# Opening norm of a two-layer encoder: sums of squares by TensorE as the input lands, scale on ScalarE, shifted tiles in PSUM

## The chip, the cores and the metric

The kernel runs on one core of a Trainium2 chip. The metric is the time of one execution on the device in microseconds (us); lower is better. The core has TensorE (PE in the profile, its weight loads PEld), VectorE (DVE), ScalarE (ACT), GpSimd (POOL) and SyncE (SP), which here only issues DMA transfers. SBUF is the working memory, PSUM the memory that TensorE writes and that VectorE and ScalarE can read and write.

## The reference, cut to what matters

Two layers; each is a half-step feed-forward network (FFN), a mixer of three branches, and another FFN. Each sub-layer starts with an RMS norm with a shift and a scale that come from a second input `c`. Only the very first of these norms, in front of the first FFN, is touched here.

```python
def rms_norm(x, gain):
    y = xf * lax.rsqrt(jnp.mean(xf * xf, axis=-1, keepdims=True) + EPS)
    return y * gain
def modulate(h, shift, scale):
    return h * (1 + scale[:, None, :]) + shift[:, None, :]
def swiglu(h, w_gate, w_up, w_down):
    return (jax.nn.silu(h @ w_gate) * (h @ w_up)) @ w_down
...
c_act = jax.nn.silu(c)
for l in range(DEPTH):
    mod = (c_act @ w_ada[l] + b_ada[l]).reshape(B, N_MOD, D_MODEL)
    h = modulate(rms_norm(x, norm_gain[l, 0]), mod[:, 0], mod[:, 1])
    x = x + 0.5 * mod[:, 2][:, None, :] * swiglu(h, ffn_w_gate[l, 0], ffn_w_up[l, 0], ffn_w_down[l, 0])
    ...
```

Sizes: 512 tokens, 1024 features, FFN width 2816, two layers, all float32.

## The kernel before, in words

Features lie on the 128 partitions, tokens along the free axis, so `x` is 8 feature tiles of 128 x 512. Float32 precision is kept in the large products by splitting both operands into a high and a low part: `hi` is the value rounded to the matmul format fp32r, `lo` the rest. A product is then three matmuls (`triple`, L117 to L122): hi x hi (L119), hi x lo and lo x hi (L120, L121).

Weights come through `wchunk` (L237): a DMA on SP's queue into `raw` (2 buffers), a cast on ScalarE into `whi` (L262, 3 buffers), and a subtraction into `wlo` (L264, 3 buffers), on VectorE or, with `lo_eng`, on GpSimd.

The modulation vectors are made by `mod_step` (L190) one 128-feature piece at a time: a DMA brings a 128 x 1024 piece of `w_ada` (4 buffers, tag `v2`), and one VectorE instruction (L196) multiplies it by the broadcast silu(c) and sums along the row, with the bias added. For the scale pieces (kind 1) a small instruction (L201) makes `apre` = (1 + scale) x gain.

The opening (L132 to L151, then `Ffn.start`, L521) goes like this:

- `c` is loaded, passed through Silu, and broadcast to 128 partitions by two f32 matmuls against ones (L144); ScalarE copies the result to SBUF (L147).
- `x` arrives in four blocks of two feature tiles. ScalarE squares each block (L140) into the buffers that later hold `whi` and `wlo`. VectorE adds the four blocks and the two halves (L526, L528), and four f32 matmuls with one column each (L531) sum over the partitions, so that the sum for each token stands on a partition.
- VectorE forms the mean (L535) and the inverse root by three Newton steps (`rsqrt`, L268), then VectorE and ScalarE write it on the diagonals of four 128 x 128 matrices (L542, L540), and one f32 matmul against ones (L544) broadcasts it to all partitions, into PSUM (`rb`).
- For each feature tile `d`: `h(d)` multiplies `rb` by `x` (L553), ScalarE writes scale and shift rounded into `hhi` (L555) and, in full, over `t` itself (L556), VectorE subtracts them into `hlo` (L557). Then the dot products for tile `d + 1` follow. `product(d, ...)` multiplies the tile with six 128 x 128 weight tiles (three of the gate and three of the up matrix, one 384 KB chunk of `w_first`): 18 matmuls into six PSUM accumulators that stay open over all eight `d`.

After that the FFN goes on weight chunk by weight chunk, with all of `hhi` and `hlo` in place.

The scheduler that turns this program into one queue per engine orders each engine's instructions by program order and by when it reckons them ready. `tc.issue_after(ins)` adds: not ahead of `ins` on its engine. `behind("vector")` does it with the instruction in `gate["vector"]`. A tile's buffer is handed on when all that used it are done. Of the 8 PSUM banks four have the tag `acc` and four `mm`.

Of the kernel before, what the change touches and what calls it, by code (L numbers as in the profile page):

```python
# [15 lines left out]
F32 = mybir.dt.float32  # L16
F32R = mybir.dt.float32r
I32 = mybir.dt.int32
AF = mybir.ActivationFunctionType
ALU = mybir.AluOpType  # L20
AX = mybir.AxisListType

P = 128
T = 512
D = 1024
# [6 lines left out]
NT = T // P  # L32
EPS = 1e-6
# [7 lines left out]
def encoder_kernel(tc, xT, c, w_ada, b_ada, gains, w_gate, w_up, w_down, w_qkv, w_f, w_ubg,  # L41
                   qk_gain, rel, fbias, w_pool, pool_scale, w_branch, w_out, inv_cnt, w_first, out):
    nc = tc.nc
# [12 lines left out]
    mm = nc.tensor.matmul  # L56
# [3 lines left out]
    def nm(s):  # L60
        uid[0] += 1
        return f"{s}_{uid[0]}"

    def st(shape, dt, tag, bufs):
        return sb.tile(shape, dt, tag=tag, bufs=bufs, name=nm(tag))

    def acc(shape=(P, T)):
        return ps.tile(list(shape), F32, tag="acc", bufs=4, name=nm("acc"))

    def mmt(shape=(P, T)):  # L70
        return ps.tile(list(shape), F32, tag="mm", bufs=4, name=nm("mm"))

    def blk(tag, dt=F32R):
        bufs = {"xv": 4, "v2": 4, "b": NB}[tag]
        return st([P, 2, T], dt, tag, bufs)

    def t1(cols=T):
        return st([P, cols], F32, "t1", 2)
# [48 lines left out]
    ones = cp.tile([P, P], F32, name="ones")  # L127
    nc.vector.memset(ones, 1.0)
    silc = [st([P, D], F32, "b", NB)]
    sil_dram = dr.tile([1, D], F32, name="sil_dram")  # L130
    crow = st([1, D], F32, "b", NB)
    nc.scalar.dma_start(crow, c)  # L132
    nc.scalar.activation(crow, crow, AF.Silu)
    x_blocks, squares, crows = [], [], []
    for b in range(4):
        xb = blk("xv", F32)
        nc.sync.dma_start(xb, xT[:, 2 * b:2 * b + 2, :])
        x_blocks.append(xb)
        sq = st([P, 2, T], F32, "wlo" if b else "whi", 3)
        nc.scalar.activation(sq, xb, AF.Square)  # L140
        squares.append(sq)
        if b < 2:
            pc = mmt()
            mm(pc, ones[0:1, :], crow[:, b * T:(b + 1) * T], start=True, stop=True)  # L144
            crows.append(pc)
    for b, pc in enumerate(crows):
        nc.scalar.copy(silc[0][:, b * T:(b + 1) * T], pc)  # L147
    badac = cp.tile([P, L, 9, KD], F32, name="badac")
    nc.sync.dma_start(badac, b_ada)
    gainc = cp.tile([P, L, 3, KD], F32, name="gainc")  # L150
# [12 lines left out]
    def late_inputs():  # L163
        for tile_, src in ((qkgc, qk_gain), (psc, pool_scale), (fbc, fbias), (icnt, inv_cnt)):
            nc.sync.dma_start(tile_, src)
        nc.sync.dma_start(sil_dram, crow)
        nc.vector.tensor_scalar(qg8, qkgc, HD ** -0.5, None, op0=ALU.mult)

    hhi = cp.tile([P, KD, T], F32R, name="hhi")
    hlo = cp.tile([P, KD, T], F32R, name="hlo")  # L170
# [6 lines left out]
    @contextlib.contextmanager  # L177
    def after(what):

        if what in last:  # L180
            with tc.issue_after(last[what]):
                yield
        else:
            yield
# [3 lines left out]
    apre = cp.tile([P, L, 3, KD], F32, name="apre")  # L188

    def mod_step(l, j, d, tag="raw"):  # L190
        raw = st([P, D], F32, tag, {"v2": 4, "raw": NRAW}[tag])
        with after("dma"):
            nc.sync.dma_start(raw, w_ada[l, j, d])
        m = modc[:, l, j, d:d + 1]
        with after("norm"):
            nc.vector.tensor_tensor_reduce(out=raw, in0=raw, in1=silc[0], scale=1.0, scalar=badac[:, l, j, d:d + 1],  # L196
                                           op0=ALU.mult, op1=ALU.add, accum_out=m)
        s, kind = divmod(j, 3)
        if kind == 1:
            g = gainc[:, l, s, d:d + 1]  # L200
            return nc.vector.scalar_tensor_tensor(apre[:, l, s, d:d + 1], m, 1.0, g, op0=ALU.add, op1=ALU.mult).ins  # L201
        if kind == 2:
            nc.vector.tensor_scalar(m, m, 0.5, None, op0=ALU.mult)

    mod_queue = [(l, j, d) for l in range(L) for j in range(9) for d in range(KD)][16:]
    mod_ptr = [0]
    mod_credit = [0.0]

    mod_tag = ["v2"]
# [15 lines left out]
    gate = {}  # L225
    quiet = [0]

    @contextlib.contextmanager
    def behind(engine):

        if engine in gate:
            with tc.issue_after(gate[engine]):
                yield
        else:
            yield

    def wchunk(src, shape, side=True, spare=None, lo_eng=None):  # L237
        if lo_eng is None:
            lo_share[1] += 1
            lo_eng = nc.gpsimd if lo_share[0] and lo_share[1] % lo_share[0] == 0 else nc.vector  # L240
        if quiet[0] > 0:
            quiet[0] -= 1
            if quiet[0] == 0:
                gate.clear()
        elif side and in_ffn[0] and mod_tag[0] == "v2":
            mod_credit[0] += MOD_RATE
            while mod_credit[0] >= 1.0:
                mod_credit[0] -= 1.0
                mod_pop()
        raw = st([P] + list(shape), F32, "raw", NRAW)  # L250
        last["dma"] = nc.sync.dma_start(raw, src).ins
        if spare == "ptb":
            both = st([P, 2] + list(shape), F32R, "ptb", 2)
            hi, lo = both[:, 0], both[:, 1]
        elif spare == "b":
            hi = st([P] + list(shape), F32R, "b", NB)
            lo = st([P] + list(shape), F32R, "b", NB)
        else:
            hi = st([P] + list(shape), F32R, "whi", 3)
            lo = st([P] + list(shape), F32R, "wlo", 3)  # L260
        with behind("scalar"):
            nc.scalar.copy(hi, raw)  # L262
        with behind("vector"):
            lo_eng.tensor_tensor(lo, raw, hi.bitcast(F32), op=ALU.subtract)  # L264
        return hi, lo
# [164 lines left out]
    class Ffn:  # L430
# [90 lines left out]
        def start(self):  # L521

            l = self.l
            sums = squares[0]
            for sq in squares[1:]:
                nc.vector.tensor_tensor(sums, sums, sq, op=ALU.add)  # L526
            ssum = st([P, T], F32, "ssum", 1)
            gate["vector"] = nc.vector.tensor_tensor(ssum, sums[:, 0, :], sums[:, 1, :], op=ALU.add).ins  # L528
            pv = mmt((P, NT))
            for t in range(NT):  # L530
                mm(pv[:, t:t + 1], ssum[:, t * P:(t + 1) * P], ones[:, 0:1], start=True, stop=True)  # L531
            with behind("vector"):
                mod_step(l, 0, 0, "v2")
            v = st([P, NT], F32, "nt_v4", 1)
            nc.vector.tensor_scalar(v, pv, 1.0 / D, EPS, op0=ALU.mult, op1=ALU.add)  # L535
            r = rsqrt(v, NT)
            dg = st([P, NT, P], F32, "ssum", 1)
            for t in range(NT):
                if t % 2:
                    nc.scalar.activation(dg[:, t, :], ident, AF.Copy, scale=r[:, t:t + 1])  # L540
                else:
                    gate["vector"] = nc.vector.tensor_scalar(dg[:, t, :], ident, r[:, t:t + 1], None, op0=ALU.mult).ins  # L542
            rb = mmt()
            mm(rb, ones, dg.rearrange("p a b -> p (a b)"), start=True, stop=True)  # L544
            pgs = [(acc(), acc()), (acc(), acc()), (mmt(), mmt())]

            with behind("vector"):
                ready = [mod_step(l, 1, 0, "v2")]
            gate.clear()

            def h(d):
                t = t1(T)
                scaled = nc.vector.tensor_tensor(t, rb, xd(d), op=ALU.mult).ins  # L553
                a, b = apre[:, l, 0, d:d + 1], modc[:, l, 0, d:d + 1]
                nc.scalar.activation(hhi[:, d, :], t, AF.Identity, scale=a, bias=b)  # L555
                nc.scalar.activation(t, t, AF.Identity, scale=a, bias=b)  # L556
                nc.vector.tensor_tensor(hlo[:, d, :], t, hhi[:, d, :].bitcast(F32), op=ALU.subtract)  # L557
                if d + 1 < KD:
                    with tc.issue_after(ready[0]):
                        mod_step(l, 0, d + 1, "v2")  # L560
                    with tc.issue_after(scaled):
                        ready[0] = mod_step(l, 1, d + 1, "v2")

            def product(d, w):
                for n in range(3):
                    for which in range(2):
                        i = 3 * which + n
                        triple(pgs[n][which], w[0][:, i, :], w[1][:, i, :], hhi[:, d, :], hlo[:, d, :],
                               d == 0, d == KD - 1)

            for d in range(KD):
                h(d)
                product(d, wchunk(w_first[d], (6, P), side=False, lo_eng=nc.gpsimd))
            gate.clear()
            late_inputs()
            return [self.act(n, *pgs[n]) for n in range(3)]

# [507 lines left out]
```

## Time and profile before

| what | value |
|---|---|
| median of 3 runs | 2505.24 us (2504.62 to 2512.64) |
| the profiled execution | 2514.29 us, its span 2512.5 us |
| TensorE busy | 2440.8 us, 97% of the span |
| weight loads (PEld) | 2039.0 us, 81% |
| VectorE busy | 1374.1 us, 55% |
| ScalarE busy | 979.7 us, 39% |
| GpSimd busy | 384.8 us, 15% |
| HBM traffic | 127 GB/s over the span |

A span runs from the first to the last instruction of the core. Matmuls are pipelined: one of 512 columns is listed with 389 ns on average, while the next begins earlier. Lines (L553) are lines of the kernel before; out<-in names the tiles written and read. The time in brackets behind a row is how long the engine stood idle in front of it and who ended that.

### The profile page before, as it was taken

The numbers are of one execution on the slowest core, as the hardware profiler recorded it, in microseconds if no ns is written. First come the engines' busy times: TensorE is split into PE (matmuls) and PEld (weight loads), VectorE is DVE, ScalarE is ACT, GpSimd is POOL, SyncE is SP. The second block draws the span as 40 slices with busy tenths as digits, with TensorE's granted clock in tenths as the row PEclk, the third lists the DMA queues.
The fourth block names the chain that finished last, engine by engine and source line by source line (L and its number), as shares of the span: only waits on it lengthen the run. The fifth ranks groups of instructions, "written<-read, shape, count | busy, mean of one in ns | idle before, by whom it ended". The sixth has DMA issues, their size and how long they took to land. (4 is left out here: it accounts for less than half of the span.)

```text
span 2512.5 us, 30820 instructions
## 1 busy us (share of the span) xinstructions
PE 2440.8 (97%) x11898; PEld 2039.0 (81%) x11898; DVE 1374.1 (55%) x2429; ACT 979.7 (39%) x1632; POOL 384.8 (15%) x369
## 2 busy tenths in 40 slices
PE   6999999999999999999999999999899999999999
PEld 5888888777788888888888888877778888888888
DVE  8655536688753365555365543367787434533332
ACT  4322235767532343222332223355766334422231
POOL 2000003243322220000020000123332322100000
PEclk9999999999999999999999999999999999999999
DMA  7655533222323335555335532323233233222322
GB/s 252 227 188 198 191 111 110 76 80 91 107 89 109 119 113 196 185 201 184 101 117 187 192 121 97 118 84 93 64 110 102 92 116 121 74 95 98 97 96 93
DMA packets 116263, 320.02 MB, mean 127 GB/s; under 512 B 11122, under 2 KB 13298, under 8 KB 116116
## 3 DMA queue, kind: packets, MB, share of 16 engines
q1 hardware_dynamic: 116114, 318.05, 37.6%
q8 instruction: 93, 1.52, 0.2%
q14 instruction: 54, 0.44, 0.1%
q10 hardware_dynamic: 2, 0.00, 0.0%
HBM read 311.64 MB, written 6.38 MB: 127 GB/s over the span
## 5 line engine op out<-in xcount | busy, mean ns | idle before, releaser
L262 ACT CAST whi<-raw 128x1024 fp32r<-128x1024 f32 (+1 forms) x395 | 411.7, 1045 | 1096.9 <-PE acc L120 421.5
L264 DVE TENSOR_TENSOR wlo<-raw,whi 128x1024 fp32r<-128x1024 f32 x339 | 419.0, 1238 | 532.2 <-ACT whi L262 520.1
L120 PE MATMUL mm<-hlo,whi 128*128 128x512 f32 x1304 | 507.8, 389 | 0.0
L121 PE MATMUL mm<-hhi,wlo 128*128 128x512 f32 x1304 | 507.7, 389 | 0.0
L119 PE MATMUL mm<-hhi,whi 128*128 128x512 f32 x1304 | 507.6, 389 | 0.0
L119 PE MATMUL acc<-b,whi 128*128 128x512 f32 (+1 forms) x960 | 359.0, 374 | 0.0
L121 PE MATMUL acc<-b,wlo 128*128 128x512 f32 (+1 forms) x960 | 357.2, 372 | 0.0
L120 PE MATMUL acc<-b,whi 128*128 128x512 f32 (+1 forms) x960 | 356.6, 372 | 0.0
L121 PEld LDWEIGHTS mm<-hhi,wlo 128*128 128x128 f32 x1304 | 245.0, 188 | 51.0
L119 PEld LDWEIGHTS mm<-hhi,whi 128*128 128x128 f32 x1304 | 245.0, 188 | 51.0
L120 PEld LDWEIGHTS mm<-hlo,whi 128*128 128x128 f32 x1304 | 245.0, 188 | 50.7
L309 POOL TENSOR_TENSOR ssum<-ssum,t 128x256 f32<-128x256 f32 (+1 forms) x45 | 53.6, 1190 | 1082.4 <-ACT t L308 1082.4
L121 PEld LDWEIGHTS acc<-b,wlo 128*128 128x128 f32 x960 | 184.6, 192 | 29.8
L120 PEld LDWEIGHTS acc<-b,whi 128*128 128x128 f32 x960 | 184.5, 192 | 29.1 <-DVE b L370 0.3
L119 PEld LDWEIGHTS acc<-b,whi 128*128 128x128 f32 x960 | 184.6, 192 | 28.9
L196 DVE CUSTOM_DVE_ANT_0 v<-v,b,badac 128x1024 f32<-128x1024 f32 x144 | 183.8, 1279 | 35.5 <-DMA v<-in_w_ada_dram 35.4
L119 PE MATMUL acc<-hhi,whi 128*128 128x512 f32 x480 | 192.0, 401 | 3.2 <-ACT hhi L555 3.2
L121 PE MATMUL acc<-hhi,wlo 128*128 128x512 f32 x480 | 190.1, 396 | 3.3 <-POOL wlo L264 3.1
L120 PE MATMUL acc<-hlo,whi 128*128 128x512 f32 x480 | 189.4, 395 | 1.5 <-DVE hlo L557 1.5
L454 DVE TENSOR_TENSOR t<-mm,t 128x512 f32<-128x512 f32 x86 | 59.4, 691 | 212.7 <-PE mm L121 208.6
L264 POOL TENSOR_TENSOR wlo<-raw,whi 128x1024 fp32r<-128x1024 f32 (+1 forms) x56 | 133.6, 2389 | 175.3 <-ACT whi L262 145.8
L119 PE MATMUL acc<-whi,hhi 128*128 128x512 f32 x336 | 138.2, 411 | 4.9 <-ACT t L642 3.7
(233 smaller groups left out, 3552.9 us busy)
## 6 DMA issues: line engine op xcount, KB each, us to landing
v<-in_w_ada_dram SPq DMA_DIRECT2D x144, 512.0 KB, 4.4
raw<-in_w_down_dram SPq DMA_DIRECT2D x88, 512.0 KB, 3.7
raw<-in_w_gate_dram SPq DMA_DIRECT2D x85, 512.0 KB, 3.4
raw<-in_w_up_dram SPq DMA_DIRECT2D x85, 512.0 KB, 3.4
raw<-in_w_ubg_dram SPq DMA_DIRECT2D x56, 512.0 KB, 3.5
raw<-in_w_qkv_dram SPq DMA_DIRECT2D x48, 512.0 KB, 3.7
raw<-in_w_branch_dram SPq DMA_DIRECT2D x24, 512.0 KB, 3.7
raw<-in_w_out_dram SPq DMA_DIRECT2D x16, 512.0 KB, 3.7
```

Source lines behind the costliest of these rows:

```text
L119: mm(o, lh, rh, start=start, stop=False)
L120: mm(o, lh, rl, start=False, stop=False)
L121: mm(o, ll, rh, start=False, stop=stop)
L196: nc.vector.tensor_tensor_reduce(out=raw, in0=raw, in1=silc[0], scale=1.0, scalar=badac[:, l, j, d:d + 1], op0=ALU.mult, op1=ALU.add, accu ...
L262: nc.scalar.copy(hi, raw)
L264: lo_eng.tensor_tensor(lo, raw, hi.bitcast(F32), op=ALU.subtract)
L309: nc.gpsimd.tensor_tensor(self.ssum[:, cols], self.ssum[:, cols], q, op=ALU.add)
L454: nc.vector.tensor_tensor(pr, pu, sg, op=ALU.mult)
```

## The change

- The two broadcasts of `c` are put in front of the squares; their copies to SBUF come between the squares.
- Each block is squared in two halves, and each half is summed over partitions by TensorE at once: four f32 matmuls of one column each per feature tile, accumulated over the eight tiles in four PSUM banks (`pvs`). The adds on VectorE are gone. VectorE reads the four banks one by one.
- Both first dot products are issued behind the diagonals (before, the first one stood behind the last add).
- In the opening, `apre` is made on ScalarE as gain x scale + gain; what the next dot products are ordered behind is the dot product itself.
- The full shifted tile is written to a PSUM tile `tb`, no longer over `t`, and `hlo` is formed from there.
- `wchunk` for a tile's weights is called before `h(d)` and no longer after it.

```diff
-    x_blocks, squares, crows = [], [], []
+    x_blocks, crows = [], []
+    for b in range(2):
+        pc = mmt()
+        mm(pc, ones[0:1, :], crow[:, b * T:(b + 1) * T], start=True, stop=True)
+        crows.append(pc)
+    pvs = [acc((P, 1)) for _ in range(NT)]
     for b in range(4):
         xb = blk("xv", F32)
         nc.sync.dma_start(xb, xT[:, 2 * b:2 * b + 2, :])
         x_blocks.append(xb)
         sq = st([P, 2, T], F32, "wlo" if b else "whi", 3)
-        nc.scalar.activation(sq, xb, AF.Square)
-        squares.append(sq)
+        for a in range(2):
+            nc.scalar.activation(sq[:, a, :], xb[:, a, :], AF.Square)
+            for t in range(NT):
+                mm(pvs[t], sq[:, a, t * P:(t + 1) * P], ones[:, 0:1], start=(b + a == 0), stop=(b == 3 and a == 1))
         if b < 2:
-            pc = mmt()
-            mm(pc, ones[0:1, :], crow[:, b * T:(b + 1) * T], start=True, stop=True)
-            crows.append(pc)
-    for b, pc in enumerate(crows):
-        nc.scalar.copy(silc[0][:, b * T:(b + 1) * T], pc)
+            nc.scalar.copy(silc[0][:, b * T:(b + 1) * T], crows[b])
...
         with after("norm"):
-            nc.vector.tensor_tensor_reduce(out=raw, in0=raw, in1=silc[0], scale=1.0, scalar=badac[:, l, j, d:d + 1],
-                                           op0=ALU.mult, op1=ALU.add, accum_out=m)
+            dot = nc.vector.tensor_tensor_reduce(out=raw, in0=raw, in1=silc[0], scale=1.0,
+                                                 scalar=badac[:, l, j, d:d + 1], op0=ALU.mult, op1=ALU.add,
+                                                 accum_out=m).ins
         s, kind = divmod(j, 3)
         if kind == 1:
             g = gainc[:, l, s, d:d + 1]
+            if in_start[0]:
+                nc.scalar.activation(apre[:, l, s, d:d + 1], m, AF.Identity, scale=g, bias=g)
+                return dot
             return nc.vector.scalar_tensor_tensor(apre[:, l, s, d:d + 1], m, 1.0, g, op0=ALU.add, op1=ALU.mult).ins
...
         def start(self):
-            sums = squares[0]
-            for sq in squares[1:]:
-                nc.vector.tensor_tensor(sums, sums, sq, op=ALU.add)
-            ssum = st([P, T], F32, "ssum", 1)
-            gate["vector"] = nc.vector.tensor_tensor(ssum, sums[:, 0, :], sums[:, 1, :], op=ALU.add).ins
-            pv = mmt((P, NT))
+            v = st([P, NT], F32, "nt_v4", 1)
             for t in range(NT):
-                mm(pv[:, t:t + 1], ssum[:, t * P:(t + 1) * P], ones[:, 0:1], start=True, stop=True)
-            with behind("vector"):
-                mod_step(l, 0, 0, "v2")
-            v = st([P, NT], F32, "nt_v4", 1)
-            nc.vector.tensor_scalar(v, pv, 1.0 / D, EPS, op0=ALU.mult, op1=ALU.add)
+                nc.vector.tensor_scalar(v[:, t:t + 1], pvs[t], 1.0 / D, EPS, op0=ALU.mult, op1=ALU.add)
             r = rsqrt(v, NT)
...
             with behind("vector"):
+                mod_step(l, 0, 0, "v2")
                 ready = [mod_step(l, 1, 0, "v2")]
...
                 nc.scalar.activation(hhi[:, d, :], t, AF.Identity, scale=a, bias=b)
-                nc.scalar.activation(t, t, AF.Identity, scale=a, bias=b)
-                nc.vector.tensor_tensor(hlo[:, d, :], t, hhi[:, d, :].bitcast(F32), op=ALU.subtract)
+                tb = mmt()
+                nc.scalar.activation(tb, t, AF.Identity, scale=a, bias=b)
+                nc.vector.tensor_tensor(hlo[:, d, :], tb, hhi[:, d, :].bitcast(F32), op=ALU.subtract)
...
             for d in range(KD):
+                w = wchunk(w_first[d], (6, P), side=False, lo_eng=nc.gpsimd)
                 h(d)
-                product(d, wchunk(w_first[d], (6, P), side=False, lo_eng=nc.gpsimd))
+                product(d, w)
             gate.clear()
+            in_start[0] = False
```

More of the change, by code (lines that the diff above doesn't have):

```diff
@@ L206, in encoder_kernel @@
     mod_ptr = [0]
+    in_start = [True]
     mod_credit = [0.0]
```

## The prediction

> **What bounds the kernel now.** I read the page first, its totals and its slices in time.
>
> ```profile
> span 2512.5 us, 30820 instructions
> PE 2440.8 (97%) x11898; PEld 2039.0 (81%) x11898; DVE 1374.1 (55%) x2429; ACT 979.7 (39%) x1632; POOL 384.8 (15%) x369
> PE   6999999999999999999999999999899999999999
> ```
>
> TensorE is busy nearly everywhere; only the first slice, where the changed code lies, has a gap worth a digit. So I cut the opening into stages with the windows view (PE, PEld, DVE, ACT, POOL busy with instruction counts, then clock, DMA share, GB/s).
>
> ```profile
> 0.00:23.12 23.12, 7.72 (x14) 3.44 (x14) 13.55 (x27) 9.80 (x13) 2.92 (x9) 1.00 0.77 269
> 23.12:32.85 9.73, 8.21 (x18) 5.95 (x19) 9.73 (x17) 5.27 (x7) 3.03 (x2) 1.00 0.84 287
> 32.85:64.66 31.81, 29.84 (x127) 23.73 (x126) 29.18 (x39) 14.57 (x20) 12.71 (x6) 1.00 0.69 233
> 64.66:160.00 95.34, 95.34 (x422) 78.97 (x421) 62.13 (x93) 30.04 (x39) 0.00 (x0) 1.00 0.59 210
> ```
>
> From 64.66 on TensorE has no gap: whatever moves the end of the opening moves the end of the kernel by as much. A matmul there costs 95.34 / 422 = 0.226 us, so the opening's eight products of 18 matmuls need 8 x 4.07 = 32.6 us. They get 64.66 - 23.12 = 41.5. The 8.9 lost are the first product (9.73 instead of 4.07, with its last twelve matmuls, from 27.57 to 32.85 below, 0.44 apart: the array at half speed, though the clock column has no record there and says 1.00) and waits later. Before 23.12 there is the norm. The timeline of the opening shows its chain (start, duration, what; in brackets the idle time before and who ended it).
>
> ```profile
> 4.37 3.78 PE L144 MATMUL mm<-b,ones 1*128 1x512 f32 x4 [4.37 <-ACT b L133]
> 10.73 1.05 ACT L147 COPY b<-mm 128x512 f32<-128x512 f32 x2
> 12.91 1.78 PEld L531 LDWEIGHTS mm<-ones,ssum 128*128 128x128 f32 x8 [6.34 <-DVE ssum L528]
> 14.82 0.16 DVE L535 TENSOR_SCALAR nt_v<-mm 128x4 f32<-128x4 f32 x1 [0.75 <-PE mm L531]
> 17.06 0.48 DVE L542 TENSOR_SCALAR ssum<-ident,nt_z 128x128 f32<-128x128 f32 x2
> 17.82 2.08 PE L544 MATMUL mm<-ssum,ones 128*128 128x512 f32 x2 [3.04 <-ACT ssum L540]
> 18.57 1.82 POOL L264 TENSOR_TENSOR wlo<-raw,whi 128x768 fp32r<-128x768 f32 x1 [16.92 <-ACT whi L262]
> 18.78 1.63 DVE L201 SCALAR_TENSOR_TENSOR apre<-modc,gainc 128x1 f32<-128x1 f32 x1
> 20.34 1.27 DVE L196 CUSTOM_DVE_ANT_0 v<-v,b,badac 128x1024 f32<-128x1024 f32 x1
> 21.54 0.68 DVE L553 TENSOR_TENSOR t<-mm,xv 128x512 f32<-128x512 f32 x1
> 23.12 2.07 PE L119 MATMUL acc<-hhi,whi 128*128 128x512 f32 x4 [3.23 <-ACT hhi L555]
> 27.57 0.80 PE L120 MATMUL acc<-hlo,whi 128*128 128x512 f32 x1 [1.52 <-DVE hlo L557]
> 50.71 0.50 PE L121 MATMUL acc<-hhi,wlo 128*128 128x512 f32 x1 [0.45 <-POOL wlo L264]
> 56.61 0.50 PE L121 MATMUL acc<-hhi,wlo 128*128 128x512 f32 x1 [1.52 <-POOL wlo L264]
> ```
>
> **Part 1, squares on TensorE: a loss.** Before, VectorE adds the squares and TensorE makes 4 f32 matmuls of one column, seen as 8 weight loads in 1.78 us: 0.2225 each. After, there are 32 such matmuls, so 64 loads: 64 x 0.2225 = 14.24 us. They stand in TensorE's queue behind the two c broadcasts, which end at 4.37 + 3.78 = 8.15; the copies that close ScalarE's share ended at 11.78, and with the same squares in halves it will be about there, so the squares wait for TensorE and not the other way. The sums are ready at 8.15 + 14.24 = 22.4, not 14.82: 7.6 us later. The four adds on VectorE that disappear were not the price; they ran while x landed.
>
> Whether those loads stay at 0.2225 depends on the clock. The windows view, cut at the clock's own 3.41 us stretches, has two pairs that tell; the second answer holds line L326 alone, the later norms' one-column matmuls.
>
> ```profile
> 54.24:57.65 3.41, 1.89 (x9) 1.24 (x8) 2.38 (x4) 1.04 (x2) 2.32 (x1) 1.00 0.48 157
> 57.65:61.06 3.41, 3.41 (x16) 2.60 (x15) 2.16 (x2) 1.22 (x2) 1.84 (x1) 1.00 0.77 297
> 890.50:893.92 3.42, 2.12 (x18) 1.91 (x18) 2.00 (x9) 1.29 (x4) 0.73 (x1) 1.00 0.49 172
> 893.92:897.33 3.41, 3.41 (x19) 3.41 (x18) 1.78 (x9) 0.82 (x2) 0.45 (x1) 0.50 0.00 1
> 890.50:893.92 3.42, 0.61 (x4) 0.52 (x4) 1.00 0.49 172
> ```
>
> With PE busy 1.89 and PEld 1.24 the next stretch keeps full clock; with 2.12 and 1.91 it falls to 0.50. Take out the 0.61 of one-column matmuls and 1.51 is left, less than 1.89: the order becomes right. So weight loads with one streamed column seem not to count as work, and I take 0.2225 throughout. The bounds are 14.24 us and half of that.
>
> The Trainium skill ("TensorE: Matmul & The Clock Gate", Part 1, What's actually happening) says the array leaves half rate after about 3.4 us of sustained activity; by that rule the stream would run twice as fast from about 8 us on. The trace agrees on the length of the stretch (3.41), but not, as the pair above reads, that weight loads are such activity; no run here shows a long stream of them. It is the first rival.
>
> **Part 2, from the sums to the first product: a gain.** From the sums to the diagonals is 17.06 - 14.82 = 2.24, from there to the broadcast's end 17.82 + 2.08 - 17.06 = 2.84: broadcast at 22.4 + 2.24 + 2.84 = 27.5. Both first dot products (L196) now stand behind the diagonals on VectorE; one of them used to fill the wait for TensorE. They issue 1.2 apart (cycle below): 22.4 + 2.24 + 0.48 + 2.4 = 27.5. Both arrive together, so L553 runs at 27.5. The scale's 1.63 us (L201: it ended when GpSimd's wlo ended, 20.4) and the third dot product ahead of L553 (20.34) are gone if the order comes out so; the scale on ScalarE hides behind L553. If the third one stays ahead, add 1.2. From L553 to the first matmul 23.12 - 21.54 = 1.58: 29.1, 6.0 later than before. Part 2 gives back 1.6 of the 7.6.
>
> **Part 3, the products: a gain of nearly the same size.** VectorE's cycle for one feature tile is:
>
> ```profile
> 34.63 0.68 DVE L553 TENSOR_TENSOR t<-mm,xv 128x512 f32<-128x512 f32 x1
> 35.23 1.27 DVE L196 CUSTOM_DVE_ANT_0 v<-v,b,badac 128x1024 f32<-128x1024 f32 x1
> 36.43 1.27 DVE L196 CUSTOM_DVE_ANT_0 v<-v,b,badac 128x1024 f32<-128x1024 f32 x1
> 36.97 2.44 POOL L264 TENSOR_TENSOR wlo<-raw,whi 128x768 fp32r<-128x768 f32 x1 [2.88 <-ACT whi L262]
> 37.64 2.31 DVE L557 TENSOR_TENSOR hlo<-t,hhi 128x512 fp32r<-128x512 f32 x1
> 39.88 0.14 DVE L201 SCALAR_TENSOR_TENSOR apre<-modc,gainc 128x1 f32<-128x1 f32 x1
> 39.95 0.68 DVE L553 TENSOR_TENSOR t<-mm,xv 128x512 f32<-128x512 f32 x1
> 601.36 2.40 POOL L264 TENSOR_TENSOR wlo<-raw,whi 128x1024 fp32r<-128x1024 f32 x1 [2.78 <-ACT whi L262]
> 602.01 0.69 DVE L793 TENSOR_TENSOR ptb<-mm,ptb 128x512 fp32r<-128x512 f32 x1
> ```
>
> It takes 39.95 - 34.63 = 5.32, against TensorE's 4.07. GpSimd's wlo, 1.82 undisturbed, waits for the running dot product (2.44), and hlo, both inputs in SBUF, then waits for it: 2.31. The last two rows show an instruction of hlo's new kind, one input in PSUM (mm): 0.69 in the middle of a GpSimd one, no wait. So after the change hlo and L553 take 0.6 each whatever GpSimd does, but the two dot products read SBUF twice and must still share with it. The cycle is 0.6 + 2.4 + 0.6 = 3.6 plus the part of 1.82 that VectorE can't cover with hlo and L553: 1.82 - 1.2 = 0.62 if GpSimd comes in after the second dot product, 1.82 if between the two. I take the middle, 1.22: cycle 4.82. The first cycle has no wlo in it (the first two are made while the sums run).
>
> TensorE's side: no wait for hlo any more (made at 27.5 + 0.6 + 2.4 + 0.6 = 31.1, while the six half-speed hhi matmuls last until 29.1 + 6 x 0.44 = 31.7), half speed until one full 3.41 us stretch has been busy, so for 3.4 to 6.8 us at a loss of half, 2.4 taken: 29.1 + 32.6 + 2.4 = 64.1 if VectorE keeps up. VectorE's side: 27.5 + 3.6 + 6 x 4.82 = 60.0 for the last L553, + 1.58 + 4.07 = 65.7. At 0.62 it would be 62.1, and TensorE's 64.1 holds; at 1.82 it is 69.3. The later end decides: 65.7, 1.0 us after today's 64.66.
>
> **Costed at nothing.** The weight tile asked for ahead: on SP's queue each w_first tile moves past two w_ada transfers, and from the third tile on those wait for a slot that a dot product frees (at 26.3 and 27.5).
>
> ```profile
> v<-in_w_ada_dram SPq DMA_DIRECT2D x144, 512.0 KB, 4.4
> ```
>
> They land 4.4 later, by 31.9, and are wanted in the second cycle, from about 31.7: covered, just. Were it not, each late tile would stretch one cycle. The two waits for wlo (0.45 and 1.52) should go, since the earlier w_first leaves wlo waiting for its buffer only, three products ahead; what is late next is VectorE. The shifted tile has one PSUM bank left (two crows, the broadcast and one pair of products use or have used the others): its next write waits for hlo, 0.6 in a cycle of 4.8, hidden.
>
> **Sum.** The profiled execution took 2514.29 us, 1.8 beyond its span; + 7.6 - 1.6 - 5.0 = +1.0 gives 2515.3. It lies 9 above the median 2505.24 of runs from 2504.62 to 2512.64; the difference carries over: 2506.2. What a measurement can tell from no change here is about 0.3%, 7.5 us.
>
> **Rivals.**
> - *The array warms up during the squares.* At half price the 64 loads take 7.1 (the four of L326 above: 0.52 / 4 = 0.13), the sums are ready at 15.3, everything is 7.1 earlier than forecast: end 58.6, 6.1 before today's, 2499.1. For it: the stream is unbroken from 4.37. Against: the 890.50 pair. Chance 0.14.
> - *GpSimd decides (slower).* wlo always falls between the two dot products: 69.3, and with the third one ahead of the first L553 70.5; +5.8, 2511.1. It is a loss from a wait of 1.05 per tile on (cycle 4.65). For it: at 36.97 GpSimd got in at the first boundary after it asked. Against: there it was after the second dot product. Chance 0.15.
> - *The PSUM route frees nothing*: the cycle stays 5.32. Then 27.5 + 7 x 5.32 + 5.65 = 70.4, +5.7, 2511. Against it stands the row at 602.01. Chance 0.06.
>
> **Numbers.** Forecast 0.60, within -0.6 and +2.7 us by the waits 0.62 to 1.5: 2504.6 to 2507.9. Rivals 0.35, others 0.05 (an order of the instructions that I don't foresee). The range takes in the first rival at 2499 and the second at 2511, widened to 2513 since one run of three already lay at 2512.6. Faster by over 0.3% needs the warm array and a short wait together: 0.05. Slower by over 0.3% needs the second rival with late transfers: 0.09. Within: 0.86.
>
> **What would show it.** In the changed profile: 64 one-column matmuls 0.22 apart ending near 22.4, VectorE idle until then; L553 first near 27.5, first product near 29; hlo at 0.68 every time, dot products stretched to between 1.9 and 3.1 instead; no wait for hlo or wlo on TensorE; the last product ending between 64 and 67. Wrong it is if the loads close up to 0.12, if the dot products never wait, or if anything changes after the opening.

## The result and the profile after

| | median | runs | against the kernel before |
|---|---|---|---|
| before | 2507.18 us | 9 (2504.62 to 2512.64) | |
| after | 2515.32 us | 9 (2512.02 to 2516.38) | 1.0027, 95% interval 1.0017 to 1.0038 |

The change makes the kernel slower, by 8.1 us or 0.3%; the forecast was +1.0 us, with 2513 as the upper end of the range. Line numbers in rows are those of each kernel; after the change, L272 is the wlo subtraction, L270 the weight cast, L199 the dot product, L148 the squares' matmul, L206 `apre` on ScalarE, L558 the hlo subtraction, L460 the Silu on the first FFN outputs.

The spans of the two profiled executions don't show the loss. The page of after begins:

```profile
span 2512.7 us, 30943 instructions
PE 2447.5 (97%) x11954; PEld 2044.4 (81%) x11954; DVE 1364.6 (54%) x2420; ACT 982.5 (39%) x1644; POOL 382.5 (15%) x369
```

The page of before (shown with the prediction) has a span of 2512.5 us. The views of cores give a mean granted clock of 0.995 for before and 0.997 for after: the profiled execution of before lost some 0.002 x 2512 = 5 us more at half rate, in stretches far behind the opening. These come and go from one execution to the next, so I measure the opening by a mark close behind it: the start of the 21st weight cast. From there to past 300 us the two kernels run in step. The mark in the timelines of before and of after (start, duration):

```profile
119.08 1.05 ACT L262 CAST whi<-raw 128x1024 fp32r<-128x1024 f32 x1 [3.89 <-issue]
```

```profile
126.05 1.05 ACT L270 CAST whi<-raw 128x1024 fp32r<-128x1024 f32 x1 [3.89 <-issue]
```

So the opening and its exit cost 126.05 - 119.08 = 6.97 us, inside the interval of the ratio (4.3 to 9.5 us). I call this number the shift of a kernel; it carries some 0.7 us of luck, since `c` lands earlier or later (its broadcast starts at 4.37 in the profile of before, 4.15 in after, 3.67 to 4.56 in the experiments). The timeline of after shows where it comes from.

```profile
4.15 3.77 PE L137 MATMUL mm<-b,ones 1*128 1x512 f32 x4 [4.15 <-ACT b L133]
...
11.29 10.38 PE L148 MATMUL acc<-ones,wlo 128*128 128x1 f32 x48
21.70 0.16 DVE L534 TENSOR_SCALAR nt_v<-acc 128x1 f32<-128x1 f32 x1 [0.27 <-PE acc L148]
...
25.43 1.85 POOL L272 TENSOR_TENSOR wlo<-raw,whi 128x768 fp32r<-128x768 f32 x1 [23.78 <-ACT whi L270]
25.55 2.82 DVE L199 CUSTOM_DVE_ANT_0 v<-v,b,badac 128x1024 f32<-128x1024 f32 x1
28.30 0.68 DVE L553 TENSOR_TENSOR t<-mm,xv 128x512 f32<-128x512 f32 x1
29.94 2.07 PE L119 MATMUL acc<-hhi,whi 128*128 128x512 f32 x4 [3.19 <-ACT hhi L555]
58.46 2.78 DVE L199 CUSTOM_DVE_ANT_0 v<-v,b,badac 128x1024 f32<-128x1024 f32 x1
62.57 1.20 PE L119 MATMUL acc<-hhi,whi 128*128 128x512 f32 x4 [0.75 <-ACT hhi L555]
66.84 0.39 PE L121 MATMUL mm<-hhi,wlo 128*128 128x512 f32 x1
68.30 0.50 PE L119 MATMUL mm<-hhi,whi 128*128 128x512 f32 x1 [1.08 <-ACT whi L270]
70.30 0.50 PE L121 MATMUL mm<-hhi,wlo 128*128 128x512 f32 x1 [1.26 <-DVE wlo L272]
```

Down to 66.84, the last matmul of the eight products, it goes the way that was forecast: the sums come 6.9 us late (21.70 against 14.82), the first product 6.8 (29.94 against 23.12), and the last product ends at 66.84 + 0.23 = 67.07 instead of 64.66: +2.4, where +1.0 was forecast. The rows at 68.30 and 70.30 are new: TensorE waits twice in the first weight chunk of the FFN, where before it had no gap. The windows view, cut at the clock's stretches (PE, PEld, DVE, ACT, POOL busy, clock, DMA share, GB/s), shows what follows from them.

```profile
64.30:67.71 3.41, 2.92 (x13) 2.06 (x11) 2.35 (x4) 2.59 (x5) 0.00 (x0) 1.00 0.15 59
67.71:71.10 3.39, 1.53 (x5) 0.97 (x6) 3.39 (x7) 2.71 (x4) 0.00 (x0) 1.00 0.02 5
71.10:74.52 3.42, 3.42 (x9) 2.64 (x8) 3.42 (x6) 0.45 (x1) 0.00 (x0) 0.50 0.93 301
```

The stretch with the waits holds 1.53 us of work, and the next one is granted half clock: 9 matmuls in a stretch where the kernel before gets about 15. Waits and half-rate stretch together are what is left of the shift, 6.97 - 2.4 = 4.6 us. Why the waits? ScalarE's timeline at the exit, of before and then of after:

```profile
61.44 0.60 ACT L452 ACTIVATE t<-acc 128x512 f32<-128x512 f32 x1 [2.57 <-PE acc L121]
61.94 1.05 ACT L262 CAST whi<-raw 128x1024 fp32r<-128x1024 f32 x1
```

```profile
64.73 0.60 ACT L460 ACTIVATE t<-acc 128x512 f32<-128x512 f32 x1 [1.54 <-PE acc L121]
65.71 0.60 ACT L460 ACTIVATE t<-acc 128x512 f32<-128x512 f32 x1 [0.39 <-PE acc L121]
66.21 0.61 ACT L377 CAST b<-t 128x512 fp32r<-128x512 f32 x1
66.72 0.60 ACT L460 ACTIVATE t<-mm 128x512 f32<-128x512 f32 x1
67.20 1.05 ACT L270 CAST whi<-raw 128x1024 fp32r<-128x1024 f32 x1
```

Before, the cast of the first FFN chunk stood right behind the first Silu and was done before TensorE wanted it at 64.66. After, the same cast stands behind three Silus that wait for the last products, and TensorE, which is done at 67.07, waits for it. It is the order that the scheduler gave the program; nothing in the diff touches these lines. I call this stretch, from the last product to where the FFN's chunks run without a wait, the exit.

### The profile page after: what moved, and what is told of

Read it like the earlier page. It is cut to its first block, busy times and chain, and to the rows that moved or that the text cites. A ratio compares the mean times of both kernels' runs of the same rounds, so it can differ in the third digit from the quotient of the medians.

```text
span 2512.7 us, 30943 instructions
## 1 busy us (share of the span) xinstructions
PE 2447.5 (97%) x11954; PEld 2044.4 (81%) x11954; DVE 1364.6 (54%) x2420; ACT 982.5 (39%) x1644; POOL 382.5 (15%) x369
## 5 line engine op out<-in xcount | busy, mean ns | idle before, releaser
L270 ACT CAST whi<-raw 128x1024 fp32r<-128x1024 f32 (+1 forms) x395 | 411.7, 1045 | 1101.8 <-PE acc L120 411.0
L272 DVE TENSOR_TENSOR wlo<-raw,whi 128x1024 fp32r<-128x1024 f32 x339 | 418.6, 1237 | 531.5 <-ACT whi L270 519.4
L199 DVE CUSTOM_DVE_ANT_0 v<-v,b,badac 128x1024 f32<-128x1024 f32 x144 | 192.3, 1337 | 40.7 <-DMA v<-in_w_ada_dram 40.3
L120 PEld LDWEIGHTS acc<-b,whi 128*128 128x128 f32 x960 | 181.6, 189 | 29.2 <-DVE b L378 0.3
L119 PEld LDWEIGHTS acc<-b,whi 128*128 128x128 f32 x960 | 181.7, 189 | 28.7
L272 POOL TENSOR_TENSOR wlo<-raw,whi 128x1024 fp32r<-128x1024 f32 (+1 forms) x56 | 131.5, 2352 | 176.6 <-ACT whi L270 138.1
```

Of the source, the lines that this page charges most:

```text
L119: mm(o, lh, rh, start=start, stop=False)
L120: mm(o, lh, rl, start=False, stop=False)
L199: dot = nc.vector.tensor_tensor_reduce(out=raw, in0=raw, in1=silc[0], scale=1.0, scalar=badac[:, l, j, d:d + 1], op0=ALU.mult, op1=ALU.add ...
```

## The experiments

My theory by now had two separate losses: the sums that come late, which the rest of the change nearly pays back (+1.0 as forecast), and the exit's order, unforeseen. The first rival: everything behind the sums is worse, PSUM tile and ScalarE's `apre` included. The second: the one-column matmuls are not slow by the clock, but by themselves. Each ratio below is against executions of the kernel before from the same session; their medians were 2509.4 to 2510.0 us.

**The adds back on VectorE**, the rest of the change kept (`e1_adds_back`).

```diff
...
-            for t in range(NT):
-                mm(pvs[t], sq[:, a, t * P:(t + 1) * P], ones[:, 0:1], start=(b + a == 0), stop=(b == 3 and a == 1))
+        squares.append(sq)
...
+            for sq in squares[1:]:
+                nc.vector.tensor_tensor(sums, sums, sq, op=ALU.add)
...
             with behind("vector"):
-                mod_step(l, 0, 0, "v2")
                 ready = [mod_step(l, 1, 0, "v2")]
```

> The changed kernel with the squares summed on VectorE again and the first dot product where it was; the scale on ScalarE, the shifted tile in PSUM and the weight tile asked for ahead stay. If the late sums are the loss (21.7 us with the change against 14.8 before): sums at 14.8, L553 first near 21, the last product ends near 59 (12.0 after the last L553, which comes 26.8 after the first), 5 to 6 us ahead of the kernel before, about 2502. If dot products that wait for GpSimd are the loss, or transfers: the cycle or the transfers hold the end at 64 or later whatever the start, and the time is that of the kernel before or above.

Measured 2502.67 us, 0.997 of before (0.9958 to 0.9983). Its timeline:

```profile
12.02 1.86 PE L536 MATMUL mm<-ones,ssum 128*128 128x1 f32 x8 [3.95 <-DVE ssum L533]
21.77 2.08 PE L119 MATMUL acc<-hhi,whi 128*128 128x512 f32 x4 [1.69 <-ACT hhi L560]
111.90 1.05 ACT L267 CAST whi<-raw 128x1024 fp32r<-128x1024 f32 x1 [3.89 <-issue]
```

The first product starts at 21.77 and the shift is 111.90 - 119.08 = -7.2 us. Without Part 1 the other parts gain. The exit's loss is gone here as well (the cast stands behind one Silu again, at 54.75, and TensorE doesn't wait for it), so this run doesn't tell the late sums from the exit; `e3_chunk_first` does. This version beats both kernels, by about 7 us against before.

**The squares' matmuls alone**, on the kernel before (`e4_squares_alone`): the first hunks of the change's diff, with both first dot products behind the diagonals.

> The kernel before with part 1 alone: squares summed by TensorE, the broadcasts ahead, both first dot products behind the diagonals; the scale on VectorE, the shifted tile in SBUF, the weight tile asked for after. If the late sums are the loss and the other parts give back about 5: sums at 21.7, L553 first at 28.3 to 30, cycle 5.3, the last product ends near 71 to 73, 7 us or more behind the kernel before, 2514 to 2517. If the other parts are what costs, it is no slower than the change's opening: end at 67 or less.

Measured 2517.94 us, 1.0029 (1.0018 to 1.004).

```profile
127.19 1.05 ACT L265 CAST whi<-raw 128x1024 fp32r<-128x1024 f32 x1 [3.89 <-issue]
```

Shift +8.1, of which +7.44 at the last product's end (72.10, in the 71 to 73 that I expected) and 0.7 at the exit, where the cast stands behind two Silus. With e1's -7.18 that makes +0.3 at the last product, where the change itself has +2.4: the two sides nearly cancel, but the parts don't simply add.

**The other three parts, each alone on the kernel before**: the PSUM tile (`e5_psum_tile_alone`), `apre` on ScalarE (`e6_scale_act_alone`), the weight tile asked for ahead (`e7_early_weight_alone`).

```diff
e5:
-                nc.scalar.activation(t, t, AF.Identity, scale=a, bias=b)
+                tb = mmt()
+                nc.scalar.activation(tb, t, AF.Identity, scale=a, bias=b)
e6:
...
+            if in_start[0]:
+                nc.scalar.activation(apre[:, l, s, d:d + 1], m, AF.Identity, scale=g, bias=g)
+                return dot
...
e7:
+                w = wchunk(w_first[d], (6, P), side=False, lo_eng=nc.gpsimd)
                 h(d)
-                product(d, wchunk(w_first[d], (6, P), side=False, lo_eng=nc.gpsimd))
+                product(d, w)
```

> The kernel before with one part: the full shifted tile in PSUM. If GpSimd's subtraction only hands its wait on: hlo takes 0.68 every time, but the small scale instruction behind it (both inputs in SBUF) then waits instead, the cycle stays 5.3 and the later weight casts move by less than 1 us. If hlo's wait is what the cycle lost: cycle 3.8 to 4.2, TensorE's waits go, 2 us or more ahead.

> The kernel before with one part: the opening's scale on ScalarE. If waits are only handed on: hlo still waits 1.6 for GpSimd in the cycles, the first L553 comes up to 1.5 earlier, the later casts move by 0 to 1.5 us. If the scale was what blocked: cycle near 4, 2 us or more ahead.

> The kernel before with one part: each weight tile of the opening asked for ahead of its feature tile. TensorE's two waits for wlo (0.45 and 1.52) should shrink, VectorE's cycle of 5.3 stays and TensorE then waits for hhi or hlo instead: between 0 and 2 us ahead. All three single parts together then give less than the 7.2 us that the three give in one kernel (the later casts of the run without the TensorE squares). If the parts simply add, the three moves sum to 7.

Measured: 0.9986 (0.9977 to 0.9996), 1.0 (0.999 to 1.001) and 0.9994 (0.9984 to 1.0003). The mark in the three timelines:

```profile
116.35 1.05 ACT L262 CAST whi<-raw 128x1024 fp32r<-128x1024 f32 x1 [3.89 <-issue]
```

```profile
116.55 1.05 ACT L267 CAST whi<-raw 128x1024 fp32r<-128x1024 f32 x1 [3.89 <-issue]
```

```profile
118.73 1.05 ACT L262 CAST whi<-raw 128x1024 fp32r<-128x1024 f32 x1 [3.89 <-issue]
```

Shifts -2.7, -2.5 and -0.35, of which up to 0.9 in the first two is `c` and `x` that landed earlier. None is a loss, so the first rival falls. Only the PSUM tile is faster than the interval's doubt. Together in one kernel (e1) the three give more than their sum, -7.2 against -5.6, since each alone leaves TensorE a wait that another one would remove: 1.50 for wlo with the PSUM tile (at 54.09), 1.40 for hlo with the scale (at 26.61), 1.55 for hlo with the early weight (at 50.83); e1 has a single gap, 0.62.

**128 columns of ones instead of one** (`e2_wide_ones`): the same number of weight loads, but each streams 128 columns.

```diff
-    pvs = [acc((P, 1)) for _ in range(NT)]
+    pvs = [acc((P, P)) for _ in range(NT)]
...
-                mm(pvs[t], sq[:, a, t * P:(t + 1) * P], ones[:, 0:1], start=(b + a == 0), stop=(b == 3 and a == 1))
+                mm(pvs[t], sq[:, a, t * P:(t + 1) * P], ones, start=(b + a == 0), stop=(b == 3 and a == 1))
...
```

> The changed kernel with 128 columns of ones in each of the 32 matmuls instead of one: the same sums, 128 times. If only streamed columns count as work for TensorE's clock, the array reaches full speed after the first 3.41 us stretch that is filled, between 11.3 and 14.7, and the rest of the 64 loads come at about 0.115: sums ready at 17 to 18.5 instead of 21.7, and the whole about 3 to 4 us faster than the change. If weight loads count alike, or the clock is not the matter, the sums come at 21.7 or later, since more columns are streamed.

Measured 2505.91 us, 0.9985 (0.9976 to 0.9994). Two rows of its windows view, then rows of its timeline:

```profile
10.60:14.00 3.40, 3.40 (x32) 3.40 (x32) 0.00 (x0) 0.86 (x2) 0.42 (x1) 1.00 1.03 415
20.80:24.20 3.40, 1.65 (x2) 0.50 (x2) 3.22 (x8) 0.69 (x2) 0.50 (x1) 0.50 0.00 0
```

```profile
7.39 3.55 PE L148 MATMUL acc<-ones,whi 128*128 128x128 f32 x16
10.78 5.52 PE L148 MATMUL acc<-ones,wlo 128*128 128x128 f32 x48
17.07 1.80 POOL L272 TENSOR_TENSOR wlo<-raw,whi 128x768 fp32r<-128x768 f32 x1 [1.69 <-ACT whi L270]
17.13 1.76 DVE L286 SCALAR_TENSOR_TENSOR nt_z<-nt_u,nt_j 128x4 f32<-128x4 f32 x1
115.71 1.05 ACT L270 CAST whi<-raw 128x1024 fp32r<-128x1024 f32 x1 [3.89 <-PE mm L120]
```

More work per matmul, and the stream is faster: 48 matmuls in 5.52 us (0.115 each) where one column took 10.38 (0.216). The pace changes within the stream: the 16 matmuls before that took 3.39 (7.39 to 10.78), 0.212 each. The clock column's 1.00 at 10.60 proves nothing by itself, since it says 1.00 for the slow stream of after too, where it has no record. But at 20.8, after TensorE has stood idle, e2 has a fall to 0.50 on record, so the clock had been full; after has none in its opening, though TensorE stands idle there as well and its first product runs at half rate. So the price is the clock, and one-column loads don't raise it: the second rival falls. Streamed columns alone don't raise it either: the `c` broadcasts, 512 columns each but from a single partition, fill e2's clock stretch from 3.75 to 7.16 (counted back from 20.80 in steps of 3.41; the broadcasts run from 3.68 to 7.46), and the next 16 matmuls are still at half rate. What else it takes, the number of rows at work for one, no run here tells. The Trainium skill ("TensorE: Matmul & The Clock Gate", Part 1, What's actually happening) says full rate follows some 3.4 us of sustained activity. By the two streams this holds only if loads with one column are no such activity: 64 of them kept the array busy for 14 us and stayed at 0.216.

The shift is -3.4, so 10.4 us better than the change, where I expected 3 to 4; 4.6 of that is the exit, whose cast stands ahead of the Silus here, at 55.33. It is not more since the earlier sums bring VectorE's small steps beside GpSimd's wlo: the step at 17.13 takes 1.76 us, from just behind the start of a wlo to its end, and a second one 1.80; such a step takes 0.16 elsewhere.

**The first FFN chunk ahead of the Silus** (`e3_chunk_first`), on the change.

```diff
...
-            return [self.act(n, *pgs[n]) for n in range(3)]
+            self.early = self.gate_up(0, 3)
+            with tc.issue_after(last["cast"]), tc.issue_after(last["sub"]):
+                return [self.act(n, *pgs[n]) for n in range(3)]
```

> The changed kernel with the cast and the subtraction of the first FFN weight chunk after the opening put ahead of the three Silu evictions on ScalarE and their products on VectorE. If the exit is a loss of its own (TensorE waits 1.08 for that cast and 1.26 for that subtraction at 68 to 70, then runs one 3.41 us stretch at half clock, 1.7 lost): both waits and the stretch go, the later weight casts stand 2.5 to 3 us behind those of the kernel before and no longer 6.97, 2511 or so. If the waits come from late products or late transfers, they stay and the time is that of the change, 2515.

Measured 2509.38 us, 0.9997 (0.9988 to 1.0006). Rows of its timeline:

```profile
29.47 2.08 PE L119 MATMUL acc<-hhi,whi 128*128 128x512 f32 x4 [3.18 <-ACT hhi L557]
61.55 1.03 ACT L270 CAST whi<-raw 128x1024 fp32r<-128x1024 f32 x1
63.41 0.60 ACT L461 ACTIVATE t<-acc 128x512 f32<-128x512 f32 x1 [0.82 <-PE acc L121]
65.47 0.39 PE L121 MATMUL mm<-hhi,wlo 128*128 128x512 f32 x1
120.12 1.05 ACT L270 CAST whi<-raw 128x1024 fp32r<-128x1024 f32 x1 [3.89 <-PE mm L120]
```

The cast is back in front (61.55, ahead of the first Silu), neither exit wait nor half-rate stretch is left, and the shift, +1.04, is all made by the last product's end: 65.47 + 0.23 = 65.70 against 64.66. The exit is shown to be a loss of its own: with it gone the interval takes in no change at all. That the shift meets the forecast's +1.0 is in part luck. I had expected 2.5 to 3 for this run; the 1.4 us by which the last product ends earlier than in after (65.70 against 67.07) are not the exit's. 0.47 of them is `c` that landed earlier; for the rest, TensorE's three gaps in the products (0.19 to 0.75) are down to one of 0.17, and why the products' order came out better I leave open.

**Filled with matmuls** (`e8_filled`): e1 and 30 matmuls of ones by ones whose result nobody reads, so that columns stream all the time.

```diff
+    def fill(ins, n):
+        with tc.issue_after(ins):
+            for _ in range(n):
+                mm(scr, ones, ones, start=True, stop=True)
+    fill(bc, 8)
...
+            fill(sm, 10)
...
+            fill(mm(rb, ones, dg.rearrange("p a b -> p (a b)"), start=True, stop=True).ins, 12)
```

> The run without the TensorE squares, with 30 matmuls of ones by ones (128 columns, results unused) put on TensorE behind the c broadcasts (8), behind the sums (10) and behind the norm's broadcast (12), so that columns stream until the first product. If streamed columns set the clock, it is full from about 11 and stays so: the first product runs at 0.23 per matmul from its start near 21.8, about 2 us more than the 7.2 are gained, 2500 to 2501. If it is not the clock, nothing is gained, and the fillers may hold the chain up.

Measured 2501.88 us, 0.9966 (0.9954 to 0.9977).

```profile
13.80:17.20 3.40, 2.81 (x14) 2.51 (x13) 3.05 (x11) 0.40 (x2) 1.48 (x1) 0.50 0.83 333
```

```profile
21.24 1.20 PE L119 MATMUL acc<-hhi,whi 128*128 128x512 f32 x4
23.85 0.50 PE L120 MATMUL acc<-hlo,whi 128*128 128x512 f32 x1 [0.95 <-DVE hlo L572]
112.44 1.05 ACT L275 CAST whi<-raw 128x1024 fp32r<-128x1024 f32 x1 [3.89 <-issue]
```

A miss: the first product runs at full rate (four matmuls in 1.20 instead of 2.08 us), but shift (-6.6) and time are e1's. The fillers had gaps, so the clock didn't stay full from 11 on but fell to half for one stretch (13.80 to 17.20) and was full again from there. TensorE, faster now in the first product, waits for hlo (0.95, later 0.29 and 1.10) and loses 0.7 at the exit. From there VectorE holds the products, and a warm array buys nothing here.

**The dot products early** (`e9_dots_early`): e3, with both first dot products while TensorE sums, where VectorE is idle.

```diff
...
+            mod_step(l, 0, 0, "v2")
+            ready = [mod_step(l, 1, 0, "v2")]
...
-            with behind("vector"):
-                mod_step(l, 0, 0, "v2")
-                ready = [mod_step(l, 1, 0, "v2")]
+            ready = [gate["vector"]]
...
```

> The change with the first FFN chunk ahead of the last Silus, as in the run before it, and both first dot products ahead of VectorE's reading of the sums, so that they run while TensorE still sums (in the change they stand behind the diagonals, and the second took 2.82 us there because it had waited for GpSimd's first wlo). Theory one, the dots hold the chain: sums at 21.3 to 21.7, broadcast of the root at 26.8, so L553 first at 26.8 to 27 instead of 28.3, and the later weight casts 0.5 to 1.5 us earlier than with the chunk order alone, where they stood 1.04 later than in the kernel before: about level with before, near 2508.5. Theory two, TensorE and the late sums alone hold it, and the third dot product takes the place of the second one ahead of L553: L553 first at 28 or later, casts as with the chunk order alone, 2509.4.

Measured 2504.36 us, 0.9983 (0.9974 to 0.9992).

```profile
11.90 1.28 DVE L199 CUSTOM_DVE_ANT_0 v<-v,b,badac 128x1024 f32<-128x1024 f32 x1
26.34 0.69 DVE L556 TENSOR_TENSOR t<-mm,xv 128x512 f32<-128x512 f32 x1 [1.16 <-PE mm L548]
27.99 2.08 PE L119 MATMUL acc<-hhi,whi 128*128 128x512 f32 x4 [1.69 <-ACT hhi L558]
117.44 1.05 ACT L270 CAST whi<-raw 128x1024 fp32r<-128x1024 f32 x1 [3.89 <-issue]
```

Theory one: the first tile is multiplied at 26.34 and waits for nothing but the broadcast; TensorE has no gap behind 27.99. Shift -1.64, so 2.7 better than e3, more than the 0.5 to 1.5 I expected. With two matters of order put right, the change as it stands, late sums and all, is slightly faster than before. The median lies further below that of before (5.0 us) than the shift; part of that lies far behind the opening, where executions differ, and I leave it open.

**Wide ones and early dot products** (`e11_wide_early`): e9 with e2's edit.

> The run before it (the change, first FFN chunk ahead of the last Silus, both first dot products ahead of the sums' reading), with 128 columns of ones instead of one, so that the sums stream. If what is left of the loss is only that the sums are late, it goes: sums read by 16.4 instead of 21.3, L553 first near 22 instead of 26.3 (21.0 if none of VectorE's small steps waits for GpSimd, as two did with the wide ones alone, 1.6 us each), first product 22.5 to 24.5 at full speed, later weight casts 5.5 to 7 us earlier than before, as with the adds back on VectorE: 2502 to 2504. The rival, that from here VectorE's cycle holds the products whatever the start, gives nothing over the run before it: 2504.4, casts 2 us earlier than before, and waits for hlo on TensorE.

Measured 2505.59 us, 0.9986 (0.9976 to 0.9996): the rival, nearly.

```profile
25.04 2.07 PE L119 MATMUL acc<-hhi,whi 128*128 128x512 f32 x4 [1.69 <-ACT hhi L558]
26.77 2.58 POOL L272 TENSOR_TENSOR wlo<-raw,whi 128x768 fp32r<-128x768 f32 x1 [8.13 <-ACT whi L270]
27.59 2.84 DVE L199 CUSTOM_DVE_ANT_0 v<-v,b,badac 128x1024 f32<-128x1024 f32 x1
41.47 0.50 PE L120 MATMUL acc<-hlo,whi 128*128 128x512 f32 x1 [0.79 <-DVE hlo L561]
116.19 1.05 ACT L270 CAST whi<-raw 128x1024 fp32r<-128x1024 f32 x1 [3.89 <-issue]
```

The first product is 3 us earlier than in e9, the mark only 1.25 (shift -2.9). wlo now falls between the two dot products in three cycles running (2.84 at 27.59, 2.86 and 2.85 in the next two), L556 follows at 30.97, 36.15 and 41.34, 5.2 apart, and TensorE waits for hlo. Here the forecast's second rival, "GpSimd decides", does hold. The code of the products is that of e9, where the spread is another: where wlo falls in VectorE's cycle hangs on when the products start, too.

## Why the prediction was wrong

**The step that failed** is the first one drawn from the windows view: "From 64.66 on TensorE has no gap: whatever moves the end of the opening moves the end of the kernel by as much". It took an exit without a gap as one that doesn't depend on the opening. It has no gap because a cast on ScalarE was done 1.7 us before TensorE wanted it (61.94 + 1.05 against 64.66); in the changed kernel that cast stands elsewhere in ScalarE's queue. By what reckoning the scheduler put it there I can't read from a trace. Under "Costed at nothing" I named what hides each edit up to the last product, and nothing for the chunk behind it. I put the exit at nothing; it cost 4.6 us. e3, which puts the cast back ahead, has neither the waits nor the half-rate stretch, and its time is that of before. I had written "Wrong it is [...] if anything changes after the opening", but with 0.05 for "an order of the instructions that I don't foresee" I gave it too little, and no size.

**Part 1 was right.** 64 loads at 0.2225 were forecast, 0.216 measured; sums at 22.4, read at 21.70. The reading of the pair at 54.24 and 890.50, that one-column loads don't count as work for the clock, is confirmed by e2. The first rival, a warm array, needs more columns than this change has. (Its 7.1 us were half of 14.24; at the 0.13 per load cited beside it they would be 8.3, at e2's 0.115 they are 7.4.)

**Part 2 gave back almost nothing**: 0.1 us (sums 6.9 late, first product 6.8) where 1.6 were forecast. From the sums to the first tile it took 28.30 - 21.70 = 6.6 instead of 5.1; that the tile came only 0.8 after the forecast 27.5 is Part 1's doing, whose sums were 0.7 earlier than forecast. The dot products behind the diagonals were put at 1.2 each; the second took 2.82, since GpSimd's first wlo started at 25.43 in between. I had "the first two are made while the sums run", but the cast for it stands on ScalarE behind the diagonals, which the late sums hold. e9 shows the size of that: both dots moved away, the first tile comes with the broadcast.

**Part 3 had the right mechanism and the wrong end**: it gave back 6.8 - 2.4 = 4.4 us, where 5.0 were forecast. hlo takes 0.68 from PSUM at every tile, the dot products take the waits instead (1.66 to 2.82), TensorE's waits for wlo are gone. e5 alone gives -2.7. From first to last L553 VectorE took 55.06 - 28.30 = 26.8 where 60.0 - 27.5 = 32.5 were forecast, but the last product did not follow its L553: the last scale's dot product, stretched to 2.78 at 58.46, held ScalarE, and TensorE waited 0.75 for hhi at 62.57. The last product's end was 67.07, 1.4 later than 65.7.

**The slower rival** (GpSimd between the dot products, 2511.1) did not decide here: TensorE has three gaps of 0.19 to 0.75 in the products, not a cycle of 5.42. e11 shows the case in which it does.

**The range** reached to the rivals I had, all inside the opening. Added up as measured: Part 1 +6.9, Part 2 -0.1, Part 3 -4.4, the exit +4.6, together the shift of 7.0. Without the exit the change would have been +2.4, inside the range.

## What to carry to other kernels

Where TensorE has no gap behind a stage, look up by how much each of its next inputs was early and on which engine's queue that input stands; that slack is what a later stage end can use up, and a scheduler may reorder the queue. A matmul with one column is priced by its weight load at the clock that it fails to raise: for the sum over partitions here, on an array at half rate, 128 columns were cheaper than one. And before moving work to TensorE because it is idle, ask for whom the engine that loses the work was late: here VectorE's adds ran while the input landed, and freed nothing.

## What the runs showed of the hardware that was not expected

- Streaming 128 columns instead of one made the same weight loads faster, 0.115 instead of 0.216 us each, because the clock rose (e2 against after). Two `c` broadcasts that stream 512 columns from one partition did not raise it.
- Two waits of 1.08 and 1.26 us within one stretch of 3.39 were enough for the next stretch to run at half clock (67.71 to 74.52). The Trainium skill ("TensorE: Matmul & The Clock Gate", Why this matters for your kernels) advises against idle gaps of more than about 3 us between bursts; here neither gap was half that long, and the array fell back all the same. What seems to count is the work in the stretch, 1.53 of 3.39 here; 1.89 of 3.41 kept full clock in the prediction's first pair.
- VectorE's instructions of 128 x 4 elements can wait for GpSimd too, 1.76 instead of 0.16 us (e2). So could the scale step of 128 x 1 elements in the kernel before (1.63 us at 18.78); in e2 it stands in the norm's own chain.
